# Down projections of two SwiGLU layers: eight half-block products per pair of blocks replaced by seven, operands streamed through DRAM, sums over all pairs in PSUM

## The chip, the cores and the metric

The kernel runs on one core of one Trainium2 chip. The metric is the device time of one execution in microseconds (us), the median of several runs. Beside the runs there is one profiled execution, from whose trace every duration below is read.

## The reference

The program is one layer of a streaming encoder for 1024 tokens of 1024 channels, all in 32-bit floats: a feed-forward network (FFN 1), a mixer (attention and a recurrence), and a second feed-forward network (FFN 2), each in a frame of normalisation, modulation, gate and residual.

```
D_MODEL = 1024; SEQ = 1024; D_FF = 2816; DEPTH = 1

def swiglu(h, w_gu, w_down):
    g, u = jnp.split(h @ w_gu, 2, axis=-1)
    return (jax.nn.silu(g) * u) @ w_down

def sandwich(x, fn, g_pre, g_post, shift, scale, gate, res_w):
    h = modulate(rmsnorm(x, g_pre), shift, scale)
    y = rmsnorm(fn(h), g_post)
    return x + res_w * gate[:, None, :] * y

def reference(...):
    mod = (c_act @ w_ada[l] + b_ada[l]).reshape(b, N_SUB, 3, D_MODEL)
    ...
    x = sandwich(x, ffn1, ..., 0.5)
    x = sandwich(x, mix, ..., 1.0)
    x = sandwich(x, ffn2, ..., 0.5)
```

The change concerns `act @ w_down` of the two FFNs: [1024 tokens, 2816] times [2816, 1024].

## The kernel before

**Precision.** Every operand of a product is split into two parts in the type fp32r: `hi`, a cast by ACT, and `lo = raw - hi`, a subtraction by DVE or GpSimd (POOL), in `split` (L135 to L137). A product is then three matmuls: hi x hi, hi x lo, lo x hi. A matmul here has 128 x 128 against 128 x 512 elements.

**Gate and up.** The hidden width 2816 is 22 blocks of 128 channels. The first 4 blocks of FFN 1 and the first 3 of FFN 2 are plain products. For each block after them `block` (L612) does seven products of half blocks in place of eight (Strassen's scheme: sums and differences of quarters of the operands are multiplied, and the results are added with signs). For every product `mix` (L582) makes a sum of two quarters of the weight block on GpSimd (`wsum`, L592; five of the seven need one), casts it on ACT (L595) and takes the rest on DVE (L596). This runs one block ahead: after product i of block fb, operand i of block fb+1 is prepared. DVE and ACT also move results out of PSUM (`sub_t` at L619 and others). The finished block of `act` is stored to DRAM (L648), in one transfer of 512 KB. The raw gate and up weights of the block after the next follow (L481, tiles `raw` and `sr`, 512 KB each). In FFN 1 one step of the modulation's matrix product (`bg`, the "adaLN" tiles `rawa`, 512 KB of weights each) runs after each block, since later parts of the program need its result.

**Down projection.** It takes the 22 blocks in seven chunks of 2, 4, 3, 3, 3, 4 and 3. For a chunk, `down_w` loads the activations and the weights of each block (tile `rawd`, 512 KB, L729) and splits them, the weights' remainders on GpSimd. Then, for each of 8 blocks of 128 tokens, all blocks of the chunk are multiplied into two PSUM banks `pd` (L766), of 512 output channels each. The first chunk's result is copied to `yacc` in SBUF (ACT, L777); the others are added to it by DVE (L779).

**Epilogue.** When a token block is complete, the class `Epilogue` treats it in stages. `put` sums its squares (ACT, L304), forms 1/rms (`rstd`, two small operations on GpSimd, L305 and L306) and multiplies by the gate (GpSimd, L365). `update` adds it to the residual (DVE, L371), stores it and takes the next sum of squares. `norm` (L382) normalises, and `drain` transposes the normalised tokens on PE for the next layer. `last_steps` says which stage runs at which step. The very last token block of the program goes through `push_last` (L407), which works in halves of 512 channels.

**What sets the order.** PE, DVE, ACT and GpSimd work their instructions in the order in which the code is written. A scheduler orders SP's queue, which issues all large DMAs, one behind the other: an instruction that waits on SP holds up all behind it. Tiles come from pools with a fixed number of buffers: 3 of `raw` (shared by all streamed weights and by `rawd`), 4 each of `wh` and `wl`, 22 of the general 512 KB tiles that `t4` returns, 16 of `h`. PSUM has 8 banks: 6 of the tag `ps` (`bank`) and 2 of the tag `tr` (`trbank`, for transposes).

## Time and profile before

| | |
|---|---|
| median of 3 runs | 2282.09 us |
| their range | 2281.98 to 2283.41 us |
| span of the profiled execution, first to last instruction | 2280.4 us |
| mean granted TensorE clock of that execution | 0.991 |
| moved by DMA in it | 250.31 MB, 110 GB/s on average |

The profile names an engine, a line, an operation and the tile it writes (`<-` the tiles it reads), with numbers of buffers left out. PE is TensorE's matmul, PEld its loading of weights, which overlaps with it. DVE is the vector engine, ACT the scalar engine, POOL is GpSimd, SP the engine whose queue issues the DMAs. The groups of instructions give, behind a count `x54:`, the least, median and largest duration in ns. A row of the timeline begins with the start and the duration in us; what stands in brackets at its end is the idle time of the engine just ahead of it and what ended that.

### The profile page before, as it was taken

Reading aid. Unit: us, or ns where it says so; the run is one execution under the profiler, and the core shown is the slowest. Engines: PE = TensorE matmul, PEld = TensorE weight load, DVE = VectorE, ACT = ScalarE, POOL = GpSimd, SP = SyncE. Lnnn points to the kernel's source line nnn. Section 1 sums busy time; section 2 is a strip of 40 time slices with the busy share of each in tenths; the row PEclk is TensorE's granted clock in tenths of the full one; section 3 lists DMA queues with packets and bytes.
Section 4 is the critical chain, followed back from the end, with each engine's and each line's share of the span. In section 5 each row is a group of like instructions: output and inputs, shape, how many; then the busy total and the mean of one; then the engine's idle time right before and its main releaser. Section 6 shows DMA issues by size and latency. Waiting matters only on the chain.

```text
span 2280.4 us, 26502 instructions
## 1 busy us (share of the span) xinstructions
PE 2212.2 (97%) x10227; PEld 1837.4 (81%) x10227; DVE 1277.7 (56%) x1830; ACT 925.0 (41%) x1473; POOL 638.2 (28%) x449
## 2 busy tenths in 40 slices
PE   5989999999999999999999999999989999999998
PEld 3867888888788788888898988887878888888886
DVE  6675565545755677643336666546864444433444
ACT  3533333342223587821147777336433333342121
POOL 3433333322225311000021120006443333322324
PEclk9999999999999999999999999999999999999999
DMA  9322333345663211245312011554322222233223
GB/s 297 101 65 75 111 111 102 111 146 177 195 211 120 77 50 40 66 148 166 113 51 65 25 59 53 165 176 169 113 81 83 84 82 83 84 121 110 93 93 120
DMA packets 217749, 250.31 MB, mean 110 GB/s; under 512 B 10864, under 2 KB 172824, under 8 KB 217624
## 3 DMA queue, kind: packets, MB, share of 16 engines
q1 hardware_dynamic: 217512, 248.60, 34.7%
q8 instruction: 80, 1.31, 0.2%
q14 instruction: 45, 0.37, 0.0%
q10 hardware_dynamic: 112, 0.03, 0.0%
HBM read 203.51 MB, written 48.23 MB: 110 GB/s over the span
## 4 chain that ended last, share of the span: by engine, by line
PE 80%; DVE 8%; ACT 4%; issue 3%; DMA 2%; POOL 2%; SPq 1%; POOLq 0%; DVEq 0%; ACTq 0%
PE pd L766 19%; PE pj L433 6%; PE pj L434 6%; PE pj L435 6%; PE pj L1064 5%; PE psB L603 3%; PE psB L604 3%; PE psB L605 3%; PE psC L603 3%; PE psC L604 3%; PE psC L605 3%; PE psA L603 3%; PE psA L604 3%; PE psA L605 3%; PE pv L1111 1%
## 5 line engine op out<-in xcount | busy, mean ns | idle before, releaser
L766 PE MATMUL pd<-dh,ah 128*128 128x512 f32 x1440 | 346.9, 392 | 0.0
L766 PEld LDWEIGHTS pd<-dh,ah 128*128 128x128 f32 x1440 | 271.8, 189 | 57.0 <-POOL dh L137 0.5
L434 PE MATMUL pj<-hl,wh 128*128 128x512 f32 x576 | 226.9, 394 | 5.5 <-DVE hl L316 5.5
L779 DVE TENSOR_TENSOR yacc<-yacc,pd 128x512 f32<-128x512 f32 x190 | 121.9, 683 | 193.3 <-PE pd L766 193.2
L435 PE MATMUL pj<-hh,wl 128*128 128x512 f32 x576 | 227.1, 394 | 2.6 <-DVE wl L137 1.9
L433 PE MATMUL pj<-hh,wh 128*128 128x512 f32 x576 | 229.3, 398 | 0.0
L592 POOL TENSOR_TENSOR wsum<-raw,sr 128x512 f32<-128x512 f32 x70 | 101.0, 1443 | 318.4 <-DVE wm L596 313.8
L596 DVE TENSOR_TENSOR wm<-wsum,wm 128x512 fp32r<-128x512 f32 x185 | 146.8, 804 | 61.9 <-ACT wm L595 59.2
L595 ACT CAST wm<-wsum 128x512 fp32r<-128x512 f32 x185 | 112.5, 620 | 111.3 <-PE psB L605 83.9
L137 POOL TENSOR_TENSOR wl<-raw,wh 128x1024 fp32r<-128x1024 f32 x25 | 61.2, 2454 | 292.0 <-ACT wh L136 246.7
L136 ACT CAST wh<-raw 128x1024 fp32r<-128x1024 f32 (+1 forms) x86 | 86.8, 1011 | 129.2 <-PE pj L434 53.2
L434 PEld LDWEIGHTS pj<-hl,wh 128*128 128x128 f32 x576 | 109.4, 190 | 29.3 <-DVE hl L316 7.4
L435 PEld LDWEIGHTS pj<-hh,wl 128*128 128x128 f32 x576 | 109.3, 190 | 26.9 <-DVE wl L137 3.2
L603 PE MATMUL psB<-hh,wm 128*128 128x512 f32 x296 | 117.2, 396 | 14.1 <-DVE mixes L619 14.1
L433 PEld LDWEIGHTS pj<-hh,wh 128*128 128x128 f32 x576 | 109.5, 190 | 22.1 <-ACT hh L321 0.3
L137 DVE TENSOR_TENSOR wl<-raw,wh 128x1024 fp32r<-128x1024 f32 (+1 forms) x61 | 73.8, 1211 | 84.7 <-ACT wh L136 84.7
L604 PE MATMUL psB<-hl,wm 128*128 128x512 f32 x296 | 116.8, 395 | 0.0
L605 PE MATMUL psB<-hh,wm 128*128 128x512 f32 x296 | 116.8, 394 | 0.0
L603 PE MATMUL psC<-hh,wm 128*128 128x512 f32 x296 | 115.6, 391 | 0.5 <-ACT wm L595 0.5
L605 PE MATMUL psA<-hs,wm 128*128 128x512 f32 x296 | 115.3, 389 | 0.4 <-DVE wm L596 0.4
L605 PE MATMUL psC<-hh,wm 128*128 128x512 f32 x296 | 115.3, 390 | 0.0
L603 PE MATMUL psA<-hs,wm 128*128 128x512 f32 x296 | 115.3, 389 | 0.0
(296 smaller groups left out, 5218.0 us busy)
## 6 DMA issues: line engine op xcount, KB each, us to landing
rawa<-in_w_ada_dram SPq DMA_DIRECT2D x56, 512.0 KB, 3.7
raw<-in_ffn_w_gu_dram SPq DMA_DIRECT2D x49, 512.0 KB, 4.0
rawd<-act SPq DMA_DIRECT2D x44, 512.0 KB, 4.3
rawd<-in_ffn_w_down_dram SPq DMA_DIRECT2D x44, 512.0 KB, 4.1
raw<-in_w_in_dram SPq DMA_DIRECT2D x44, 512.0 KB, 3.8
sr<-in_ffn_w_gu_dram SPq DMA_DIRECT2D x39, 512.0 KB, 5.7
act<-act SPq DMA_DIRECT2D x37, 512.0 KB, 4.2
rawa<-in_w_ada_dram SPq DMA_DIRECT2D x32, 256.0 KB, 5.6
```

What stands on the lines that cost most here:

```text
L137: (eng or nc.vector).tensor_tensor(lo, raw, hi.bitcast(F32), op=ALU.subtract)
L433: nc.tensor.matmul(dst, wh[:, kk, :], xhk[:, sl], start=first, stop=False)
L434: nc.tensor.matmul(dst, wh[:, kk, :], xlk[:, sl], start=False, stop=False)
L435: nc.tensor.matmul(dst, wl[:, kk, :], xhk[:, sl], start=False, stop=last)
L595: nc.scalar.copy(t[:, 0], src)
L596: nc.vector.tensor_tensor(t[:, 1], src, t[:, 0].bitcast(F32), op=ALU.subtract)
L603: nc.tensor.matmul(dst, t[:, 0, kk, :], xh, start=first and kk == 0, stop=False, skip_group_check=True)
L604: nc.tensor.matmul(dst, t[:, 0, kk, :], xl, start=False, stop=False, skip_group_check=True)
L605: nc.tensor.matmul(dst, t[:, 1, kk, :], xh, start=False, stop=last and kk == 3, skip_group_check=True)
L766: nc.tensor.matmul(pd[h], a_[:, tk], w_[:, h * 512 : (h + 1) * 512], start=(i == 0 and j == 0), stop=(i == n - 1 and j == 2),)
L779: nc.vector.tensor_tensor(yacc[sb][:, sl], yacc[sb][:, sl], pd[h], op=ALU.add)
L1064: nc.tensor.matmul(d, a[:, k, :], b[k][:, sl], start=k == 0 and i == 0, stop=k == KB - 1 and i == 2)
```

## The change

The down projection is now done like the gate and up products: the 22 blocks are taken as 11 pairs, and the two halves of a pair's channels, of the tokens and of the output channels make 2 x 2 blocks, so that seven products of halves stand for eight (numbered 1 to 7, in the order `STREAM`). For each product the contraction runs over all 11 pairs in PSUM: 4 banks hold 4 token blocks x 512 output channels, each bank receiving 3 matmuls of every pair. One "unit" is a tile `rawd` of 128 x 2 x 512 elements: the product's half of the activations and its half of the weights, 256 KB each, loaded by two DMAs (L789) and split by one cast and one subtraction. There are 7 x 11 = 77 units per FFN; `take` requests them three ahead.

Four of the seven products need sums or differences of `act` (rows of a pair against each other and halves of tokens), four need sums of `w_down`. `pair_sums` makes them ahead of the products: two loads of 512 KB, four additions on GpSimd of 128 x 512 elements (L756) and two stores of 512 KB into new DRAM tensors, `acts` and `downs`. `all_sums` lists them, the weights of a pair and then the activations of pairs that are complete, as a generator with a `yield` after the loads and after each addition. One step of it runs after each product of `block` (behind `mix`), the rest with the first product of the down projection.

Products 1, 6, 7 and 4 accumulate in one set of four banks (`chain`, two of them of the tag `tr`) which are read between them without being cleared, so that the next product adds to the one before; products 2, 5 and 3 have banks of their own. `reads` says which results ACT copies and DVE adds to `yacc`. In the last product the first four units are multiplied for all token blocks, while the Epilogue treats token blocks 0 to 3; the last seven units are kept in `t4` tiles and taken for one token block after the other.

```diff
-CHUNKS = (2, 4, 3, 3, 3, 4, 3)
+KEPT_FROM = 4
...
     def trbank(name):
+        if tr_home[0] == "ps":
+            return bank(name)
...
         def push_last(self, sb, y, pd):
...
-            for h, sl in enumerate(halves):
-                junk = tmp[0].tile([P, D], BF16, tag="junk", bufs=2, name=nm("junk"))
-                nc.vector.tensor_tensor(y[:, sl], y[:, sl], pd[h], op=ALU.add)
-                nc.scalar.activation(junk[:, sl], y[:, sl], AF.Square, scale=D ** -0.5, accum_out=sq[h])
-                if h == 0:
-                    nc.vector.tensor_tensor(y[:, sl], y[:, sl], g[:, sl], op=ALU.mult)
+            one = halves[1]
+            nc.scalar.activation(junk[1][:, one], y[:, one], AF.Square, scale=D ** -0.5, accum_out=sq[1])
+            nc.vector.tensor_tensor(y[:, one], y[:, one], g[:, one], op=ALU.mult)
             self.update(sb - 1)
+            one = halves[0]
+            nc.scalar.activation(junk[0][:, one], pd, AF.Square, scale=D ** -0.5, accum_out=sq[0])
+            nc.vector.tensor_tensor(y[:, one], pd, g[:, one], op=ALU.mult)
...
-            nc.vector.tensor_tensor(y[:, halves[1]], y[:, halves[1]], g[:, halves[1]], op=ALU.mult)
...
                 def after(i):
                     mix(fb + 1, i)
-                    if fb == NF - 1 and i in (6, 5, 4, 3):
-                        down_w(0, (6, 5, 4, 3).index(i))
+                    next(jobs, None)
+                    if fb == NF - 1 and i in (5, 4, 3):
+                        units.fetch((5, 4, 3).index(i) + 1)
+
+                ready[0] = fb
...
-                bg(1)
+                bg(2)
+            ready[0] = NF
...
+        def pair_sums(j, weights):
+            src, dst = (w_down, down_s) if weights else (act_d, act_s)
+            top, bot = t4("top"), t4("bot")
+            nc.sync.dma_start(top, rows(src, 2 * j))
+            nc.sync.dma_start(bot, rows(src, 2 * j + 1))
+            t1, t2, b1, b2 = top[:, h1], top[:, h2], bot[:, h1], bot[:, h2]
+            add, sub_ = ALU.add, ALU.subtract
+            yield
+            if weights:
+                steps = ((t1, t2, t1, sub_), (t2, b2, t2, sub_), (b2, b2, t1, sub_), (b1, b1, b2, sub_))
             else:
+                steps = ((b2, t2, b2, add), (t2, t1, t2, sub_), (t1, b2, t1, sub_), (b1, b1, t1, sub_))
+            for o, p, q, op in steps:
+                nc.gpsimd.tensor_tensor(o, p, q, op=op)
+                yield
+            nc.sync.dma_start(rows(dst, 2 * j), top)
+            nc.sync.dma_start(rows(dst, 2 * j + 1), bot)
...
+                    raw = wpool.tile([P, 2, 512], F32, tag="raw", bufs=3, name=nm("rawd"))
+                    for o, (t, k, half) in enumerate((act_of[p], down_of[p])):
+                        nc.sync.dma_start(raw[:, o], rows(t, 2 * j + k)[:, (h1, h2)[half]])
+                    if p == STREAM[-1] and j >= KEPT_FROM:
+                        hi, lo = t4("dh", F32R, (P, 2, 512)), t4("dl", F32R, (P, 2, 512))
+                    else:
+                        hi, lo = (wpool.tile([P, 2, 512], F32R, tag=t, bufs=4, name=nm("dh")) for t in ("wh", "wl"))
+                    split(raw, hi, lo, nc.gpsimd if self.n > 8 and self.n % 3 == 2 else nc.vector)
...
+            for p in STREAM[:-1]:
+                own = p in (1, 6, 7)
+                dst = chain if own else [bank("pv") for _ in range(4)]
+                for j in range(PAIRS):
+                    ops = units.take(p, j, 3)
+                    for i in range(half):
+                        mm(dst[i], i, ops, j == 0 and p not in (6, 7), j == PAIRS - 1)
+                    if own:
+                        next(jobs, None)
+                        next(jobs, None)
+                        bg(1)
...
+            for j in range(KEPT_FROM):
+                ops = units.take(p, j, 3)
+                for i in range(half):
+                    mm(chain[i], i, ops, False, False)
+                epi.put(j, yacc[j])
+                if j > 0:
+                    epi.update(j - 1)
+                if j > 1:
+                    epi.norm(j - 2)
+
+            last_steps = {4: ((3,), (2, 3), 2), 5: ((4,), (), 4), 6: ((5,), (4,), 2), 7: ((6,), (5,), KB)}
+            for i in range(half):
+                sb = half + i
+                for j in range(KEPT_FROM, PAIRS):
+                    mm(chain[i], i, units.take(p, j, 3), False, j == PAIRS - 1)
+                if tail and i == half - 1:
+                    epi.push_last(sb, yacc[sb], chain[i])
+                    break
+                copy(sb, h1, chain[i])
+                epi.put(sb, yacc[sb])
...
```

In the two listings of before and after below, a row is one instruction: its line, the operation, the tile with its number that it writes, and what it reads. GpSimd's queue in the gate and up blocks of FFN 2, before: the five weight sums of one block and the first of the next.

```order
L592 TENSOR_TENSOR wsum_13949<-raw_13929 128x512
L592 TENSOR_TENSOR wsum_13967<-raw_13929,sr_13931 128x512
L592 TENSOR_TENSOR wsum_14005<-sr_13931,raw_13929 128x512
L592 TENSOR_TENSOR wsum_14023<-sr_13931 128x512
L592 TENSOR_TENSOR wsum_14060<-raw_13929,sr_13931 128x512
L592 TENSOR_TENSOR wsum_14086<-raw_14066 128x512
```

And with the change (the line of the weight sums is now L598, that of the pair sums L756):

```order
L598 TENSOR_TENSOR wsum_14511<-raw_14491 128x512
L756 TENSOR_TENSOR bot_14429<-bot_14429,top_14428 128x512
L598 TENSOR_TENSOR wsum_14530<-raw_14491,sr_14493 128x512
L756 TENSOR_TENSOR top_14537<-top_14537 128x512
L598 TENSOR_TENSOR wsum_14575<-sr_14493,raw_14491 128x512
L756 TENSOR_TENSOR top_14537<-bot_14538,top_14537 128x512
L598 TENSOR_TENSOR wsum_14594<-sr_14493 128x512
L756 TENSOR_TENSOR bot_14538<-bot_14538,top_14537 128x512
L756 TENSOR_TENSOR bot_14538<-bot_14538 128x512
L598 TENSOR_TENSOR wsum_14633<-raw_14491,sr_14493 128x512
```

An addition of a pair now stands ahead of nearly every weight sum, in the same queue; the five weight sums of a block are still in their order.

SP's queue at the same place, before: per block one store of `act` and two loads of weights.

```order
L648 DMA act_11949<-act_13796 128x1024
L481 DMA sr_14068<-in_ffn_w_gu_dram 128x8x128
L481 DMA raw_14340<-in_ffn_w_gu_dram 128x8x128
L648 DMA act_11949<-act_13933 128x1024
L481 DMA sr_14205<-in_ffn_w_gu_dram 128x8x128
```

With the change (L758 and L759 store a pair's sums, L746 and L747 load the two rows of a pair, L487 loads the gate and up weights, L654 stores the block):

```order
L758 DMA acts_12139<-top_14428 128x1024
L759 DMA acts_12139<-bot_14429 128x1024
L487 DMA sr_14493<-in_ffn_w_gu_dram 128x8x128
L487 DMA raw_14794<-in_ffn_w_gu_dram 128x8x128
L654 DMA act_12138<-act_14346 128x1024
L746 DMA top_14537<-in_ffn_w_down_dram 128x1024
L747 DMA bot_14538<-in_ffn_w_down_dram 128x1024
L758 DMA downs_12140<-top_14537 128x1024
L759 DMA downs_12140<-bot_14538 128x1024
L746 DMA top_14640<-in_ffn_w_down_dram 128x1024
L747 DMA bot_14641<-in_ffn_w_down_dram 128x1024
L487 DMA sr_14647<-in_ffn_w_gu_dram 128x8x128
```

The loads of a pair stand behind the stores of the pair before and, every second or third time, behind two weight loads and the block's store; the weight loads in turn stand behind stores, which wait for GpSimd's additions.

GpSimd's queue at the end of FFN 1's down projection, before: squares and gate products of the token blocks, with no split between them.

```order
L365 TENSOR_TENSOR yacc_3710<-yacc_3710,gate_4295 128x1024
L305 TENSOR_SCALAR rstd_5128<-rstd_5128 128x1
L306 TENSOR_TENSOR rstd_5128<-rstd_5128,nhalf 128x1
L365 TENSOR_TENSOR yacc_3733<-yacc_3733,gate_4295 128x1024
L305 TENSOR_SCALAR rstd_5136<-rstd_5136 128x1
```

With the change (L309 and L310 form `rstd`, L369 is the gate product, L141 the split; `dl_5423` and `dl_5503` are the remainders of units 5 and 8 of the last product):

```order
L369 TENSOR_TENSOR yacc_4249<-yacc_4249,gate_3545 128x1024
L309 TENSOR_SCALAR rstd_5415<-rstd_5415 128x1
L310 TENSOR_TENSOR rstd_5415<-rstd_5415,nhalf 128x1
L141 TENSOR_TENSOR dl_5423<-rawd_5419,dh_5422 128x1024
...
L369 TENSOR_TENSOR yacc_4251<-yacc_4251,gate_3545 128x1024
...
L369 TENSOR_TENSOR yacc_4253<-yacc_4253,gate_3545 128x1024
L309 TENSOR_SCALAR rstd_5484<-rstd_5484 128x1
L310 TENSOR_TENSOR rstd_5484<-rstd_5484,nhalf 128x1
L141 TENSOR_TENSOR dl_5503<-rawd_5499,dh_5502 128x1024
```

Two splits that the last product's matmuls need now stand between the gate products of token blocks 0 to 3.

More of the change, by code (lines that the diff above doesn't have):

```diff
@@ new lines, in all_sums @@
+        def all_sums():
+            done = 0
+            for j in range(PAIRS):
+                yield from pair_sums(j, True)
+                while done < PAIRS and 2 * done + 2 < ready[0]:
+                    yield from pair_sums(done, False)
+                    done += 1
+            while done < PAIRS:
+                if 2 * done + 1 < ready[0]:
+                    yield from pair_sums(done, False)
+                    done += 1
+                else:
+                    yield
+        jobs = all_sums()
@@ L739, in down_phase @@
+        units = Units()
         def down_phase(make, ahead):
             epi = Epilogue(sub, xin, xout, EPS, make)
[L741 removed]
             half = SB // 2
[L743 to L752 removed]
@@ new lines, in down_phase, with mm, copy @@
+            tail = make is None
+            def mm(dst, i, ops, first, last):
+                hi, lo = ops
+                tk = slice(i * P, (i + 1) * P)
+                for n, (a_, w_) in enumerate(((hi, hi), (hi, lo), (lo, hi))):
+                    nc.tensor.matmul(
+                        dst, a_[:, 0, tk], w_[:, 1, :], start=first and n == 0, stop=last and n == 2,
+                        skip_group_check=True,
+                    )
+            yacc = {}
+            def copy(sb, sl, src):
+                if sb not in yacc:
+                    yacc[sb] = t4("yacc")
+                nc.scalar.copy(yacc[sb][:, sl], src)
```

127 lines of the change are left out of this document (53 added, 74 removed).

## The prediction

> **What bounds the kernel now.** I read the busy shares first, then the chain of work that ended last, then the stretches of the two down projections.
>
> ```profile
> PE 2212.2 (97%) x10227; PEld 1837.4 (81%) x10227; DVE 1277.7 (56%) x1830; ACT 925.0 (41%) x1473; POOL 638.2 (28%) x449
> ...
> PE 80%; DVE 8%; ACT 4%; issue 3%; DMA 2%; POOL 2%; SPq 1%; POOLq 0%; DVEq 0%; ACTq 0%
> ```
>
> TensorE (PE) is busy nearly throughout and holds 80% of the chain. The table of windows and the chain in order of time show the down projections themselves:
>
> ```profile
> 495.00:725.00 230.00, 227.55 (x1011) 188.00 (x1010) 139.16 (x152) 61.63 (x76) 70.82 (x40) 0.99 0.57 184
> 1739.00:1758.00 19.00, 19.00 (x86) 15.73 (x85) 9.22 (x14) 6.08 (x11) 6.74 (x6) 1.00 0.27 84
> 2040.00:2270.00 230.00, 230.00 (x1015) 189.99 (x1013) 95.34 (x120) 52.41 (x63) 74.33 (x41) 1.00 0.31 105
> ```
> ```profile
> 2030.57 235.17 PE pd L766 x1037
> ```
>
> After the stretch come its length, then busy time of PE, weight loads, DVE, ACT and GpSimd (POOL), the granted clock, DMA share and GB/s. The down products run without a gap, 1037 in 235.17 us, so 0.227 us each. Fewer of them is time gained, as long as nothing new makes PE wait. The second row is one 19 us block of the gate and up products: PE is full there too, and GpSimd is busy 6.74 us of 19.
>
> **What goes.** Each of the two FFNs had 22 x 8 x 2 x 3 = 1056 down products and gets 7 x 11 x 4 x 3 = 924 of the same shape. That is 264 fewer, at 0.227 us: **-59.9 us**. Everything else is cost.
>
> **Pair sums beside the gate and up blocks.** The new sums (L756 in the changed kernel) put 88 additions per FFN on GpSimd: one after each product in four products of five, in the queue that makes the weight sums of the next block. The timeline gives that queue for one block, then the ACT casts that wait for it:
>
> ```profile
> 1757.73 1.29 POOL L592 TENSOR_TENSOR wsum<-raw,sr 128x512 f32<-128x512 f32 x1 [5.18 <-DVE wm L596]
> 1760.09 1.29 POOL L592 TENSOR_TENSOR wsum<-raw 128x512 f32<-128x512 f32 x1 [1.06 <-DVE wm L596]
> 1766.05 1.29 POOL L592 TENSOR_TENSOR wsum<-raw,sr 128x512 f32<-128x512 f32 x1 [4.67 <-DVE wm L596]
> 1768.68 1.68 POOL L592 TENSOR_TENSOR wsum<-sr,raw 128x512 f32<-128x512 f32 x1 [1.34 <-DVE wm L596]
> 1770.31 1.28 POOL L592 TENSOR_TENSOR wsum<-sr 128x512 f32<-128x512 f32 x1
> ```
> ```profile
> 1774.67 0.62 ACT L595 CAST wm<-wsum 128x512 fp32r<-128x512 f32 x1
> 1777.70 0.62 ACT L595 CAST wm<-wsum 128x512 fp32r<-128x512 f32 x1 [2.41 <-PE psB L605]
> ```
>
> The sum that starts at 1768.68 ends 4.3 us ahead of its cast, the next one 6.1 us. GpSimd may be about 6 us late before anybody notices; beyond that ACT and DVE, which take their queues in order, evacuate PSUM late, and PE waits. That wait exists already at the first blocks:
>
> ```profile
> PE psB L603 <- DVE mixes L619: 14.1, 3, 6.6
> ```
>
> Now the work of a block. It has 7 products, so 7/5 = 1.4 pairs with 5.6 additions, and 5 weight sums: 10.6 x 1.29 = 13.7 us of 19.05 (84 products at 0.227). Into the rest, 5.4 us, must go two things: waits for loads, and the quarrel with DVE. The first addition of a pair waits for loads that SP issues only behind the stores of the pair before, and often behind two weight loads and the store of the block (the order above). Their durations, from the list of DMA issues and a window at the start:
>
> ```profile
> raw<-in_ffn_w_gu_dram SPq DMA_DIRECT2D x49, 512.0 KB, 4.0
> rawd<-act SPq DMA_DIRECT2D x44, 512.0 KB, 4.3
> ...
> sr<-in_ffn_w_gu_dram SPq DMA_DIRECT2D x39, 512.0 KB, 5.7
> ```
> ```profile
> 20.00:30.00 10.00, 4.64 (x14) 3.43 (x14) 7.48 (x9) 2.16 (x3) 4.50 (x2) 1.00 1.17 290
> ```
>
> A 512 KB load lands 4 us after its issue; one that is issued right behind another 1.7 us later (5.7 against 4.0), and 512 KB at 290 GB/s also take 1.8 us. So from the last addition of a pair to the first of the next: at best 4.3 us (one load), about 7 us behind a store (4.3 and the store, the second load), some 11 us behind two weight loads and a store more. One or two weight sums, 1.8 us on average, fill part of it. Per block that is 1.4 x (4.3 - 1.8) = 3.5 us at the low end and 1.4 x (6.7 - 1.8) = 6.9 us at the high one (6.7 is my mean over the orders of the pairs); I take the middle, 5.2.
>
> The quarrel is shown where GpSimd works back to back, at the start of the second FFN:
>
> ```profile
> 1613.33 2.40 POOL L527 TENSOR_TENSOR bot<-hh,hl 128x1024 f32<-128x1024 f32 x1 [4.91 <-DVE hl L316]
> ...
> 1624.10 2.85 POOL L527 TENSOR_TENSOR bot<-hh,hl 128x1024 f32<-128x1024 f32 x1
> ```
> ```profile
> 1627.42 2.89 DVE L544 TENSOR_TENSOR hs<-hsum,hs 128x512 fp32r<-128x512 f32 x1
> ...
> 1633.63 0.68 DVE L554 TENSOR_TENSOR bot<-bot,top 128x512 f32<-128x512 f32 x1
> ```
>
> A DVE operation of 0.68 us takes 2.9 us while GpSimd runs, and GpSimd's takes 2.85 instead of 2.40: about 0.4 us for each meeting. A block has 8 DVE operations on two SBUF operands; none to all of them meet GpSimd, 0 to 3.2 us, and I take half, 1.6. The sum is 13.7 + 5.2 + 1.6 = 20.5 us, 1.45 over the block. The 21 pairs that are summed in the blocks take 105 steps, 15 blocks: 15 x 1.45 = 22 us, less the 6 us of slack: **+16 us** in the second FFN. The first also moves two adaLN weight tiles per block, in the same DMA queue and through DVE; half a load (0.9 us) more per block gives 2.35 x 15 - 6 = **+29 us**. Both ends: nothing (13.7 + 3.5 = 17.2 fits), and 15 x (13.7 + 6.9 + 3.2 - 19.05) - 6 = 65 us for each.
>
> [...] If every meeting happens, the block is 22.1 us, and that is the third rival.
>
> **The first product of the first FFN** streams 11 operand tiles while 12 adaLN tiles still run between them; before, they were spread over longer steps:
>
> ```profile
> 645.00:660.00 15.00, 15.00 (x68) 12.43 (x67) 11.92 (x13) 4.22 (x4) 3.37 (x2) 1.00 0.79 252
> 660.00:675.00 15.00, 14.12 (x57) 11.54 (x56) 8.96 (x9) 5.15 (x5) 6.17 (x3) 0.77 0.67 226
> ```
>
> With the last pair and the last store it is 28 transfers of 512 KB; at 1.7 us 47.6 us of DMA. PE needs them in 30 us and the prefetch begins some 8 us ahead: **+8 us** (from 0, if enough has landed earlier, to 20 at the 226 GB/s of the second row). The other five inner products need 0.5 MB in 2.7 us, 193 GB/s, which the before ran at without PE waits; their ACT casts (1.05 of 2.72 us) and subtractions are covered by it. Cost nothing.
>
> **The last product** holds the epilogue, in 30 us instead of some 50. Its durations:
>
> ```profile
> L136 ACT CAST dh<-rawd x54: 1044/1053/1062, 477.6 to 2210.6; 128x1024 fp32r<-128x1024 f32 x54
> ...
> L137 DVE TENSOR_TENSOR ah<-rawd,ah x34: 1212/1219/3303, 500.2 to 2190.8; 128x1024 fp32r<-128x1024 f32 x34
> L137 POOL TENSOR_TENSOR dl<-rawd,dh x22: 2375/2408/3480, 486.4 to 2211.7; 128x1024 fp32r<-128x1024 f32 x22
> ```
> ```profile
> L305 POOL TENSOR_SCALAR rstd<-rstd x47: 219/426/1316, 6.7 to 2268.4; 128x1 f32<-128x1 f32 x47
> L306 POOL TENSOR_TENSOR rstd<-rstd,nhalf x47: 567/570/1673, 7.0 to 2269.4; 128x1 f32<-128x1 f32 x47
> L371 DVE SCALAR_TENSOR_TENSOR xr<-yacc,rstd,xr x15: 1272/1283/1286, 703.4 to 2273.3; 128x1024 f32<-128x1024 f32 x15
> ```
> ```profile
> L777 ACT COPY yacc<-pd x32: 589/590/592, 498.2 to 2052.6; 128x512 f32<-128x512 f32 x32
> L304 ACT ACTIVATE junk<-yacc x15: 1055/1058/1060, 698.8 to 2267.1; 128x1024 bf16<-128x1024 f32 x15
> L304 ACT ACTIVATION_READ_ACCUMULATOR junk<-yacc x15: 186/187/189, 699.8 to 2268.1; 128x1 f32 x15
> L365 POOL TENSOR_TENSOR yacc<-yacc,gate x14: 2339/2400/2419, 700.9 to 2269.9; 128x1024 f32<-128x1024 f32 x14
> L382 DVE TENSOR_SCALAR yacc<-xr,rstd x8: 745/761/2866, 710.9 to 770.1; 128x1024 f32<-128x1024 f32 x8
> ...
> L419 DVE TENSOR_TENSOR yacc<-yacc,gate x1: 2143/2143/2143, 2270.7 to 2270.7; 128x512 f32<-128x512 f32 x1
> ```
>
> Count from its first matmul. PE passes four units (10.9 us), then takes the last seven for one token block at 0.68 us each: unit 8 is due at 13.6 and that block ends at 15.7. GpSimd has ahead of unit 8's subtraction (first FFN): four puts of 0.43 + 0.57 + 2.40 = 3.4, three updates of 1.0, unit 5's subtraction and its own, 2.4 each: 21.4 us. It begins at 2.3, after a cast and a square (1.05 + 1.06 + 0.19), and ends at 23.7. Unit 10's buffer is free when unit 7 is cut at about 20.7, behind an update that waits for GpSimd; load 4.3, cast, subtraction: 27.3. The token block ends at 27.7, 12 us late. The transposes right behind it wait for copy 0.59, square 1.25, put 3.4, update 1.0, normalisation 0.76: 7 us. **+19 us**. In the second FFN no update runs on GpSimd, but half of unit 8's load stands behind a store that waits for an update (16.2): load, cast, subtraction give 24, unit 10 24.4, the token block 24.9: **+9 us**. The rest of the epilogue follows at PE's pace. Bounds: 5 less each if the queues meet better, 8 more each if loads queue as above. The final block no longer has the 2.14 us multiplication on its way to the end: **-2 us** (0 to -4).
>
> **Clock.** In the window 660 to 675 above PE sat idle for 0.9 us, the granted clock fell to 0.77 and 57 matmuls were done instead of 68: 11 x 0.227 = 2.5 us, 1.6 beyond the idle time. Three long waits: **+5 us**. [...]
>
> **Sum.** -59.9 + 16 + 29 + 8 + 19 + 9 - 2 + 5 = +24 us on a span of 2280.4: 2304; the runs' median (2282.09) lies 1.7 above that execution: **2306 us**.
>
> **Rivals.** Forecast (58%): GpSimd sets the pace of the blocks. First rival, on the other side (27%): the loads land early enough, a block's GpSimd work fits into 19.05 us, and the pair sums cost nothing: 2306 - 45 = 2261. For it speaks the 12 us that GpSimd is idle in a block now; against it that SP has the loads behind stores that wait for GpSimd itself. It decides at 5.4 us of waits and meetings per block. Second (5%): the last and first products hide their waits too: 2261 - 33 = 2228. Third (10%): every meeting and the long waits: up to 65 in place of 16 and 29: 2306 + 85 = 2391 at the most, half of it 2348. That the products aren't fewer is out: the order has 264 PE rows less.
>
> **Numbers.** A measurement of this kernel tells about 0.2% from no change, 2277.5 to 2286.7. The forecast's own spread, some 25 us, puts 0.05 of its 0.58 below and 0.06 within; the first rival 0.25 and 0.02. Faster 0.35, same 0.08, slower 0.57. The range runs from below the first rival's price to the middle of the third's: 2250 to 2365.
>
> **What would show it.** Right: in the blocks POOL is over 85% busy or waits for the DMAs of top and bot, blocks take 20 to 21 us, and PE waits for mixes or wm; two waits near the first FFN's last product, one of 9 us in the second's. Wrong: blocks of 19.1 us, or no PE wait for dl; then a term above is hidden.

## The result, and the profile after

The changed kernel takes **2391.48 us** (median of 4 runs, 2391.02 to 2392.31) against 2282.75 us of the kernel before (4 runs): 1.0478 times as long, 95% interval 1.0466 to 1.0491. The profiled execution spans 2390.5 us, 110 us more than the 2280.4 before. The forecast was 2306, range 2250 to 2365: the direction is right, the time lies outside the range, and close to the third rival's upper end (2391).

The busy shares and the chain of the changed kernel:

```profile
PE 2201.8 (92%) x9963; PEld 1813.3 (76%) x9963; DVE 1335.8 (56%) x1740; ACT 997.9 (42%) x1538; POOL 896.2 (37%) x621
...
PE 55%; DMA 13%; POOL 11%; DVE 9%; ACT 5%; issue 5%; SPq 2%; POOLq 0%; DVEq 0%; ACTq 0%
```

There are 264 matmuls fewer, as the change says, but PE is busy only 10.4 us less instead of 59.9. Its share of the chain falls from 80% to 55%, and DMA and GpSimd now hold 24%. What PE waits for, the largest rows and those that the text needs (engine, tile and line, what ended the wait; total us, times, longest):

```profile
PE psB L609 <- DVE mixes L625: 72.0, 23, 7.0
PE pc L204 <- DVE acc L191: 18.7, 3, 9.3
PE px L813 <- ACT dh L140: 10.8, 3, 5.0
PE px L813 <- POOL dl L141: 10.8, 4, 4.7
...
PE pb L134 <- DMA rowsB<-in_lru_lambda_dram: 7.7, 1, 7.7
...
PE px L813 <- DVE dl L141: 5.9, 3, 4.2
...
PE pt L339 <- DVE yacc L386: 6.3, 1, 6.3
```

In the kernel before, the first of these rows was 14.1 us. The stages, read off the starts of PE's matmuls by their tiles (us; a product of 132 matmuls at 0.227 us is 29.9):

| stage | before | after |
|---|---|---|
| FFN 1, 16 steps from a seven-product block to the next | 319.2 | 383.1 |
| FFN 1, first three down products | | 50.0, 33.5, 38.6 |
| FFN 1, first down matmul to the first seven-product block of FFN 2 | 1164.9 | 1178.5 |
| FFN 2, 17 such steps | 331.9 | 379.5 |
| FFN 2, last down product | | 45.2 |
| FFN 2, first down matmul to the end | 249.9 | 232.8 |

The steps differ by +63.9, +13.6, +47.6 and -17.1; with 2 us in the stretches between, that is the 110. The gain is there: in FFN 2 six of the seven down products run at 29.9 us each, full (first row below: stretch, its length, PE, weight loads, DVE, ACT, POOL busy, clock, DMA share, GB/s). The seventh is not (second row), nor is the down projection of FFN 1 as a whole (third row):

```profile
2157.60:2337.10 179.50, 179.50 (x794) 148.63 (x793) 73.62 (x65) 76.06 (x79) 53.88 (x24) 1.00 0.63 206
2337.10:2382.30 45.20, 33.74 (x132) 25.57 (x131) 20.70 (x15) 18.31 (x27) 32.34 (x24) 0.85 0.55 190
561.40:834.00 272.60, 233.68 (x989) 189.39 (x988) 122.03 (x108) 109.44 (x129) 92.02 (x57) 0.91 0.63 206
```

**The blocks.** The 16 blocks of FFN 2 from the second on, before and after, in the same columns:

```profile
1687.70:1992.30 304.60, 304.60 (x1345) 252.33 (x1344) 147.57 (x225) 97.34 (x176) 108.46 (x80) 1.00 0.28 83
```
```profile
1767.30:2119.50 352.20, 321.62 (x1346) 261.05 (x1345) 191.06 (x225) 100.47 (x176) 224.63 (x157) 0.96 0.56 186
```

A block takes 352.2 / 16 = 22.0 us instead of 19.04. GpSimd's waits in those 16 blocks after the change, then ACT's largest, then what SP waits for longest:

```profile
POOL bot L756 <- DMA bot<-act: 42.3, 8, 7.3
POOL wsum L598 <- DMA sr<-in_ffn_w_gu_dram: 37.7, 11, 6.4
POOL top L756 <- DMA top<-in_ffn_w_down_dram: 21.2, 7, 3.4
POOL wsum L598 <- DVE wm L602: 18.2, 10, 4.7
POOL top L756 <- DMA bot<-in_ffn_w_down_dram: 3.2, 3, 1.6
```
```profile
ACT wm L601 <- POOL wsum L598: 157.7, 56, 7.4
```
```profile
SPq L758 <- POOL top L756: 122.4, 19, 10.9
SPq L759 <- POOL bot L756: 66.2, 19, 5.9
```

Per block GpSimd works 14.0 us, waits 4.2 for the loads of a pair (`top`, `bot`), 2.4 for the weights `sr`, 1.1 for DVE and 0.2 for its own issue: 21.9 of 22.0. ACT waits 157.7 us for GpSimd's weight sums, 9.9 per block. And SP stands for 188.6 of the 352.2 us before stores (L758, L759) whose sums GpSimd has not finished. One stall step by step, first the queue of SP (start, us, what it issues), then one row each of GpSimd, ACT, DVE and PE:

```profile
1843.78 0.78 SPq L747 DMA_DIRECT2D bot<-act  x1
1856.38 0.32 SPq L758 DMA_DIRECT2D acts<-top  x1
1859.78 0.32 SPq L759 DMA_DIRECT2D acts<-bot  x1
1860.15 0.43 SPq L487 DMA_DIRECT2D sr<-in_ffn_w_gu_dram  x1
```
```profile
1865.03 1.27 POOL L598 TENSOR_TENSOR wsum<-raw,sr 128x512 f32<-128x512 f32 x1 [3.57 <-DMA sr<-in_ffn_w_gu_dram]
```
```profile
1866.33 0.62 ACT L601 CAST wm<-wsum 128x512 fp32r<-128x512 f32 x1 [4.22 <-POOL wsum L598]
```
```profile
1867.59 0.68 DVE L625 TENSOR_TENSOR mixes<-psB,mixes 128x512 f32<-128x512 f32 x1
```
```profile
1868.42 0.47 PE L609 MATMUL psB<-hh,wm 128*128 128x512 f32 x1 [2.95 <-DVE mixes L625]
```

From 1844.6 to 1859.8 SP stands, but for the 0.3 us that issue the first, before two stores that wait for GpSimd's additions; these had themselves to wait for the load of `bot`, until 1850.85. Behind the stores stands the load of `sr`, which GpSimd needs next. GpSimd starts on it 4.9 us after its issue; the weight sum, its cast, the remainder and, behind it in DVE's queue, the evacuation of `psB` are all late, and PE stands for 2.95 us. GpSimd holds up its own load. And the stall goes on after its end:

```profile
1865.00:1869.90 4.90, 1.95 (x10) 1.31 (x9) 1.99 (x3) 1.48 (x3) 1.53 (x2) 1.00 0.99 372
1869.90:1873.30 3.40, 3.40 (x10) 2.63 (x9) 1.89 (x2) 0.25 (x1) 3.32 (x3) 0.50 0.03 12
```

For the next 3.4 us the granted clock is 0.50: 8 matmuls start, 0.43 us apart (the row's 10 count two that began before it), instead of 15 at 0.227 us, which is 1.6 us lost. Nine gaps of PE in FFN 2's blocks, of 2.1 to 6.5 us, are each followed by such a stretch, of 3.4 or 6.8 us; a tenth, of 2.0 us, is not.

### The profile page after: what moved, and what is told of

The parts are those of the page before. It is cut to its first block, busy times and chain, and to the rows that moved or that the text cites. A ratio compares the mean times of both kernels' runs of the same rounds, so it can differ in the third digit from the quotient of the medians.

```text
span 2390.5 us, 27027 instructions
## 1 busy us (share of the span) xinstructions
PE 2201.8 (92%) x9963; PEld 1813.3 (76%) x9963; DVE 1335.8 (56%) x1740; ACT 997.9 (42%) x1538; POOL 896.2 (37%) x621
## 4 chain that ended last, share of the span: by engine, by line
PE 55%; DMA 13%; POOL 11%; DVE 9%; ACT 5%; issue 5%; SPq 2%; POOLq 0%; DVEq 0%; ACTq 0%
PE px L813 7%; PE pv L813 6%; PE pj L437 6%; PE pj L438 6%; PE pj L439 6%; PE pj L1150 5%; POOL wsum L598 3%; POOL bot L756 3%; DMA sr<-in_ffn_w_gu_dram 2%; POOL top L756 2%; DMA bot<-act 2%; DMA rawa<-in_w_ada_dram 2%; PE pv L1197 1%; DMA top<-in_ffn_w_down_dram 1%; DVE wm L602 1%
## 5 line engine op out<-in xcount | busy, mean ns | idle before, releaser
L602 DVE TENSOR_TENSOR wm<-wsum,wm 128x512 fp32r<-128x512 f32 x185 | 174.6, 952 | 177.3 <-ACT wm L601 176.2
L140 ACT CAST dh<-rawd 128x1024 fp32r<-128x1024 f32 x154 | 161.8, 1052 | 263.7 <-PE pv L813 69.0
L141 DVE TENSOR_TENSOR dh<-rawd,dh 128x1024 fp32r<-128x1024 f32 x100 | 131.0, 1312 | 230.5 <-ACT dh L140 230.4
L609 PE MATMUL psB<-hh,wm 128*128 128x512 f32 x296 | 128.4, 434 | 72.0 <-DVE mixes L625 72.0
L141 POOL TENSOR_TENSOR dh<-rawd,dh 128x1024 fp32r<-128x1024 f32 x40 | 96.0, 2400 | 260.2 <-ACT dh L140 260.2
L813 PE MATMUL px<-dh,dh 128*128 128x512 f32 x592 | 186.3, 396 | 1.1 <-DVE dh L141 1.1
L141 POOL TENSOR_TENSOR wl<-raw,wh 128x1024 fp32r<-128x1024 f32 x25 | 61.3, 2459 | 291.2 <-ACT wh L140 246.2
L813 PE MATMUL pv<-dh,dh 128*128 128x512 f32 x528 | 162.9, 389 | 2.2 <-POOL dh L141 1.4
L813 PE MATMUL px<-dh 128*128 128x512 f32 x352 | 142.8, 406 | 10.8 <-ACT dh L140 10.8
L598 POOL TENSOR_TENSOR wsum<-raw,sr 128x512 f32<-128x512 f32 x70 | 104.9, 1498 | 113.2 <-DMA sr<-in_ffn_w_gu_dram 71.7
L813 PEld LDWEIGHTS px<-dh,dh 128*128 128x128 f32 x592 | 113.9, 193 | 25.5 <-DVE dh L141 1.5
L609 PEld LDWEIGHTS psB<-hh,wm 128*128 128x128 f32 x296 | 61.5, 208 | 94.4 <-issue 81.7
L141 DVE TENSOR_TENSOR wl<-raw,wh 128x1024 fp32r<-128x1024 f32 (+1 forms) x61 | 76.1, 1249 | 89.8 <-ACT wh L140 89.8
```

Source lines behind the costliest of these rows:

```text
L140: nc.scalar.copy(hi, raw)
L141: (eng or nc.vector).tensor_tensor(lo, raw, hi.bitcast(F32), op=ALU.subtract)
L598: nc.gpsimd.tensor_tensor(src, p, q, op=op)
L602: nc.vector.tensor_tensor(t[:, 1], src, t[:, 0].bitcast(F32), op=ALU.subtract)
L609: nc.tensor.matmul(dst, t[:, 0, kk, :], xh, start=first and kk == 0, stop=False, skip_group_check=True)
L813: nc.tensor.matmul(dst, a_[:, 0, tk], w_[:, 1, :], start=first and n == 0, stop=last and n == 2, skip_group_check=True,)
```

## The experiments

In the code changes below, `...` stands for lines left out. Three theories on the blocks. **Q**: GpSimd waits for loads that stand in SP's queue behind stores, and those wait for GpSimd. **W**: GpSimd's added work and its meetings with DVE fill the block. **T**: the added bytes delay the loads. Times are medians beside 2282 to 2284 us of the kernel before on the same chip, with ratio and 95% interval.

**e1_no_sums.** `jobs` is empty, and the products read `act_d` and `w_down`.

```diff
...
-        jobs = all_sums()
+        jobs = iter(())
```

> Left out: all pair sums (their loads, additions and stores); the products read halves of act and of w_down in their place, so traffic and matmuls of the down projection itself stay. The blocks of gate and up cost 64 us (first FFN) and 48 us (second) more in the changed kernel than before. If the pair sums are the whole reason, the blocks go back to 19.0 us each and the time falls by 112 us and some 10 us more in the first product, to about 2270 us. If two steps of adaLN per block or something else in the blocks takes part, the first FFN's blocks stay above 20 us and the time above 2300.

2300.64 us (1.0075, 1.0046 to 1.0104), the second of the two cases. The 17 steps of FFN 2 are back to 333.5, but the 16 of FFN 1 take 341.0, not 319.2. So the pair sums cost 46 us in FFN 2 and 42 in FFN 1; another 22 us in FFN 1 come from something else, and of the down projection's losses nearly all stay (first three products 44.0, 35.8 and 36.7; last of FFN 2 47.7).

**e2_traffic_only.**

```diff
-            for o, p, q, op in steps:
-                nc.gpsimd.tensor_tensor(o, p, q, op=op)
+            for _ in steps:
                 yield
```

> Left out: the additions of the pair sums; their loads and stores stay, with nothing between. Theory Q (SP's queue: GpSimd waits for loads that stand behind stores which wait for GpSimd) and theory W (GpSimd's own work and its meetings with DVE fill the blocks) both expect the blocks near 19.0 us, since no store waits for GpSimd and GpSimd has no additions: 2270 to 2290 us. Theory T (the added bytes alone delay the weight loads): blocks stay above 20 us, over 2330 us.

2296.83 us (1.0060, 1.0037 to 1.0083), 7 us above the range given, since FFN 1 keeps what e1 left open; 340.1 and 331.6 us in the blocks, as in e1. All loads and stores of the sums are there and cost the blocks nothing. T falls.

**e3_apart.**

```diff
-                nc.gpsimd.tensor_tensor(o, p, q, op=op)
+                nc.gpsimd.tensor_tensor(own[0][:, h1], own[0][:, h2], own[0][:, h2], op=op)
...
```

> The loads and stores of the pair sums stay, with nothing between them, and GpSimd makes the same number of additions of the same size at the same places, but on a tile of its own that is loaded once: work and traffic of the changed kernel, without the dependence of one on the other (the sums are not formed). Theory Q: blocks near 19 to 19.5 us, 2275 to 2310 us. Theory W: the blocks stay at 20 to 22 us, 2360 us or more.

2300.64 us (1.0074, 1.0048 to 1.0100); 344.2 and 331.2 us. This number of additions and this traffic, without the dependence, are nearly free. In the 16 blocks of FFN 2 GpSimd now waits for nothing but DVE, which means that it is ahead:

```profile
POOL wsum L598 <- DVE wm L602: 111.8, 54, 5.2
```

W does not fall by this alone: an addition on the tile of its own, which reads one operand twice, takes 1.09 us, and GpSimd works 189.0 us in these blocks instead of the changed kernel's 224.6. The full work comes in e5.

```profile
L756 POOL TENSOR_TENSOR own<-own 128x512 f32<-128x512 f32 x75 | 81.8, 1090 | 1.3
```

**e4_ahead.** The pair's loads move in front of the additions of the pair ahead of it.

```diff
+            nxt = choose()
+            while nxt or todo[False] < PAIRS:
+                cur, nxt = nxt, choose()
+                yield
+                if cur:
+                    yield from pair_sums(*cur)
...
```

> Nothing left out. The loads of a pair are issued before the additions of the pair ahead of it, instead of behind its stores; activations go before weights where both are there. Theory Q: GpSimd's waits for top and bot (64 us in the second FFN's blocks, 43 in the first's) go, those for sr (38 and 34), which still stand behind stores, stay in part: 2310 to 2345 us. Theory W: within 10 us of 2391.

2354.80 us (1.0312, 1.0282 to 1.0342): two fifths of the way from 2391 to 2300, in the direction of Q, though 10 us more than I gave it. In FFN 2 the 17 steps are 349.1; in FFN 1 374.7. In the 16 blocks of FFN 2 the waits for the pairs fall from 66.7 to 8.2 us, and the wait for `sr` has grown from 37.7 to 55.4, since the stores still stand ahead of it:

```profile
POOL wsum L598 <- DMA sr<-in_ffn_w_gu_dram: 55.4, 14, 10.7
POOL bot L757 <- DMA bot<-act: 8.2, 2, 5.2
```

**e5_act_stores.** e4, and a pair's stores leave from ACT's queue, two products after the last addition.

```diff
-            nc.sync.dma_start(rows(dst, 2 * j), top)
-            nc.sync.dma_start(rows(dst, 2 * j + 1), bot)
+                nc.scalar.dma_start(rows(dst, 2 * j), top)
+                nc.scalar.dma_start(rows(dst, 2 * j + 1), bot)
...
```

> As e4 (loads one pair ahead), and the stores of the pair sums are issued by ACT, two products after their last addition, so that no store in SP's queue waits for GpSimd. Theory Q: GpSimd's waits for sr (58 us in e4's second FFN blocks) go too, the 17 blocks of the second FFN take 331 to 336 us (349 in e4), the 16 of the first 340 to 348 (375), and the time is 2298 to 2315 us, the level of e1 to e3. Rival: the stores only move the wait to ACT, which then casts and evacuates late: blocks stay above 20 us, 2340 or more.

2312.26 us (1.0123, 1.0094 to 1.0153): 331.1 us in FFN 2 and 348.6 in FFN 1, within a us of what Q gave. The 16 blocks of FFN 2:

```profile
1729.50:2034.10 304.60, 304.60 (x1346) 252.30 (x1345) 195.42 (x225) 98.91 (x176) 222.17 (x156) 1.00 0.61 207
```

GpSimd makes the same operations as in the changed kernel (156 against 157) in nearly the same time, 1.42 and 1.43 us each; in the blocks before it was 1.36. DVE makes 225 operations in all three, in 147.6 us before, 191.1 after the change and 195.4 here. So the whole work and the meetings with DVE are there, and PE is full, at 19.04 us per block: W falls. **Q is shown** in FFN 2, where the pair sums cost nothing now: their price was the order of stores and loads in one queue. From the changed kernel to e5 the steps of the two FFNs lose 34.5 and 48.4 us. Of the 12 us by which e5 lies above e1, 8 are in FFN 1's steps and 5 in FFN 2's first down product (34.8 us). The stores on ACT's queue without the earlier loads were not run.

**e6_last.** The last product alone; the updates, normalisations and transposes of the steps behind it are shifted to match.

```diff
-... nc.gpsimd if self.n > 8 and self.n % 3 == 2 else nc.vector)
+... nc.gpsimd if self.n > 8 and self.n % 3 == 2 and p != STREAM[-1] else nc.vector)
-                ops = units.take(p, j, 3)
+                ops = units.take(p, j, 3 + 2 * j)
-                if j > 0:
-                    epi.update(j - 1)
                 if j > 1:
-                    epi.norm(j - 2)
+                    epi.update(j - 2)
...
```

> The changed kernel with another last product: all its splits on DVE, its units requested up to seven ahead, and updates and normalisations of token blocks 0 to 3 one to two steps later. If the wait for units 5 to 10 (splits behind gate products on GpSimd, loads behind stores that wait for updates) is what makes the two last products 60.5 and 45.2 us, they become some 48 and 33 us, and the time 2362 to 2372 us. If the epilogue's own work sets their length, the waits move behind the last matmuls and the time falls by less than 8 us.

2381.08 us (1.0425, 1.0394 to 1.0455), 10 us less; expected were 19 to 29. FFN 2's last product falls from 45.2 to 34.4 us, as expected, but the time from the last matmul to the end rises from 8.1 to 15.2. In FFN 1 the product falls by 4.7 (60.6, with transposes, to 55.9). PE's waits in the tile `px` fall from 28.6 to 12.2 us, those for the normalised tokens rise from 6.3 to 10.6:

```profile
PE pt L339 <- DVE yacc L386: 10.6, 3, 5.8
PE px L813 <- ACT dh L140: 5.6, 4, 2.6
PE px L813 <- DVE dl L141: 5.2, 8, 1.1
PE px L813 <- DVE dh L141: 1.4, 1, 1.4
```

Both theories are half right: the units waited as I said, and behind them stands the epilogue's own chain.

**e7_spread.** The two adaLN steps of a block apart.

```diff
+                    if i in (4, 7):
+                        bg(1)
-                bg(2)
```

> The changed kernel with its two adaLN steps per block apart: one after product 4, one after product 7, instead of both at the block's end. If the short distance between a load or a sum and the PE instruction that needs it is the reason (PE waits of 18.7 us for acc and 7.7 us for rowsB), these waits fall below 8 us in all; the blocks of the first FFN get 10 to 22 us shorter, as far as GpSimd's waits do not hide it: 2368 to 2382 us. If adaLN costs by its work on DVE or its bytes, nothing changes: within 5 us of 2391.

2386.50 us (1.0448, 1.0418 to 1.0479), where the other theory put it. PE's waits for `rowsB` and for adaLN sums in the blocks are gone, but FFN 1's steps are only 6.6 us shorter (376.5), since PE now waits there longer for `mixes` (45.8 us, 34.9 before the edit); and in the first down product one adaLN sum still holds PE for 13.7 us.

**e8_all.** e5, e6 and e7 together.

> e5, e6 and e7 together. If the three losses are separate, their gains add: 2300 to 2315 less 20 to 28 for the last products less 10 to 20 for adaLN, 2252 to 2285 us; what is then left over 2222 (the time before less 60) is the first product and the first block.

2274.65 us (0.9965, 0.9945 to 0.9984), inside the range. With GpSimd in time, the spread of e7 is worth 22 us: FFN 1's steps go from 348.6 in e5 to 326.3, 7 above the kernel before. Work and bytes are the same in both, so these 22 us are the two adaLN steps taken back to back. (The same background queue `bg` also brings `rowsB`, parameters of the mixer.) In e5's steps PE waits 4.0 us for `rowsB`, 5.0 for an adaLN sum and 5.6 for the two parts of another, and is busy 7.9 us longer than in e8, whose PE has none of these waits. That these are the 22 us which e1 left open is likely, since size and place agree; e1 with the steps apart was not run. The last 7 us stay open.

**e10_bg_later.** The changed kernel, with no adaLN step in the first down product; they follow from the second on, one in three units.

```diff
                         next(jobs, None)
+                    if p != 1 and j % 3 == 1:
                         bg(1)
```

> The changed kernel, with no adaLN step in the first product of the down projection; from the second product on one follows every third unit. If the adaLN tiles (their turns in the DMA queue, in the three raw buffers and on PE) make the first three products of the first FFN 50.0, 33.5 and 38.6 us, these become 30 to 36 us each and the time 2364 to 2376 us. If the pair sums and operands alone do it, the three stay above 40, 33 and 33 us, and the time within 8 us of 2391.

2385.20 us (1.0449, 1.0428 to 1.0470), less gain than expected. The first product falls from 50.0 to 35.5, as the first theory has it, the next two are 32.0 and 36.8, but the fourth and fifth rise from 29.9 to 36.5 and 34.8. So 14.5 us of the first product come with the adaLN steps, and most of the cost follows them to wherever they go.

**e9_best.** e8 with that, and the sums of the last pair at one step per unit, through the first two products.

> e8 with the adaLN steps of e10, and with the last pair's sums at one step per unit through the first two products, so that ACT's store does not wait for a pair just loaded (ACT idle for 10.6 us behind GpSimd in e8's second FFN, whose first product is 34.8 us). The first three products of the first FFN fall from 45.7, 35.0 and 38.7 us to 30 to 35 each, the first of the second to 30: 2243 to 2260 us against 2274.65. If the operands' own loads set the first product, 2262 or more.

2266.24 us (0.9933, 0.9916 to 0.9949), 6 us above the range given. The first products of FFN 1 and 2 are 30.9 and 29.9, as expected; the second to fifth of FFN 1 are 34.2, 36.3, 36.8 and 36.6.

**e11_rawa.** e9 with adaLN tiles of the down projection in the general buffers.

```diff
-            raw = wpool.tile([P, 1024], F32, tag="raw", bufs=3, name=nm("rawa"))
+            raw = t4("rawa") if ada_home[0] == "t4" else wpool.tile([P, 1024], F32, tag="raw", bufs=3, name=nm("rawa"))
```

> e9, with the adaLN tiles of the down projection in the general tiles instead of in the three raw buffers that the operands use. In e9 the second to fifth product of the first FFN take 34.2, 36.3, 36.8 and 36.6 us and a unit's chain (issue, load of 3 to 6 us, cast, subtraction) holds its raw buffer for 8 to 10 us, about three units of 2.72 us. If a raw buffer lent to adaLN is what the units lack, the four fall to 30 to 32 us and the time to 2242 to 2254 us. If the DMA's bytes or DVE's time set them, they stay above 33 us and the time above 2258.

2250.54 us (0.9862, 0.9843 to 0.9880), inside the range of the buffer theory. Three of the four products fall as expected: they are 30.4, 39.3, 29.9 and 31.8. DMA moves more, not less, in the same stretch, e9 first, then e11:

```profile
530.00:590.00 60.00, 56.16 (x248) 44.31 (x246) 28.18 (x22) 21.11 (x23) 15.75 (x7) 1.00 0.67 216
```
```profile
530.00:590.00 60.00, 57.07 (x239) 46.77 (x239) 26.11 (x23) 21.80 (x23) 16.69 (x7) 0.91 0.88 290
```

So 216 GB/s was no limit, and a lent raw buffer was what the units of three products lacked. The third product does not wait for a unit at all. Its row, and PE's only wait in it:

```profile
564.40:603.60 39.20, 36.49 (x150) 30.07 (x149) 18.16 (x17) 14.28 (x16) 10.88 (x5) 0.87 0.84 273
```
```profile
PE pc L206 <- DVE yacc L845: 2.7, 1, 2.7
```

The matmuls of an adaLN step (`pc`) wait for a DVE addition that reads a result of the second product; in the down projection `pc` takes its PSUM bank from the same six as the products, so it is probably the bank that they wait for. The row's mean granted clock is 0.87, from which I estimate about 5 us more (0.13 x 39.2).

**e12_kept.** e11 with `KEPT_FROM = 5`, the updates and normalisations shifted to match.

> e11, with five units instead of four taken for all token blocks ahead of those kept in the last product. If the last products (55.7 and 37.4 us in e9) still wait for the kept units' loads and splits, 2.7 us more of cover shorten each by 2 to 5 us: 3 to 10 us below e11. If they wait for the epilogue (residual tiles, normalisation), nothing is gained: within 3 us of e11, or some us slower.

2250.22 us (0.9853, 0.9836 to 0.9869), the same as e11. The last products are 4.7 and 4.8 us shorter (52.4 and 32.4), and the tail is 5.3 longer (16.8): as in e6, the epilogue ends last. e11 and e12 beat both kernels, 1.4 to 1.5% faster than the one before, with intervals clear of 1.

## Why the prediction was wrong, step by step

**Right.** The products: 29.9 us each where nothing else interferes, so -59.9 was there to be had. The final block, -2: the end after the start of the last matmul is 8.1 us, 10.8 before. That GpSimd becomes the bound of the blocks, through loads behind stores. That this alone decides between faster and slower is not borne out: without any pair sums, e1 is still 0.75% slower than the kernel before. Of the signs named, PE's waits for `mixes` and `dl` and GpSimd's for `top` and `bot` are there; the blocks are longer than the 20 to 21 us given.

The terms beside -59.9, and what the stages show for them (us; the clock's +5 has no stage of its own):

| term | forecast | measured |
|---|---|---|
| FFN 2, steps of the blocks | +16 | +47.6 |
| FFN 1, steps of the blocks | +29 | +63.9 |
| FFN 1, first down product | +8 | +20.1 |
| FFN 1, second and third | 0 | +3.6, +8.7 |
| FFN 1, last product and what follows, up to FFN 2 | +19 | +11 |
| FFN 2, last product | +9 | +15.3 |
| final block | -2 | -2.7 |

**The term of the pair sums: the step that failed.** Forecast for GpSimd were 20.5 us per block: 13.7 of work, 1.6 of meetings with DVE, 5.2 of waits for the loads of a pair. Work and meetings measure 14.0, and the waits for `top` and `bot` 4.2, inside the stated 3.5 to 6.9. What the sum put at nothing is the other half of the loop: the weights `sr` stand behind the same stores, and GpSimd waits for them 2.4 us per block. It also waits 1.1 us for DVE: it can prepare only as many sums as `wsum` has buffers (2), so time in which it is ahead isn't saved for a later wait. With 0.2 of its own issue that makes 22.0 us, 2.96 over the old block instead of 1.45. That the waits for loads are 6.5 in all, near the 5.2, is luck. "The 6 us of slack" were a second mistake, taken off the sum once but seen nowhere: the third seven-product block of FFN 2 takes 24.1 us already. 16 x 2.96 = 47 stands against +16 in FFN 2. In FFN 1 the pair sums cost 42 (e1) against the same 16; the other 13 of the +29 stood for adaLN.

The meetings were put on the wrong engine. Their price is DVE's: its 225 operations take 43.5 us more in the 16 blocks, 2.7 per block, and e5 shows that DVE has room for it.

**AdaLN in the blocks had the wrong cause.** Half a load (0.9 us) more per block, 13 us in all, was my price for the adaLN tiles in FFN 1. The size is 22 us, and the reason another one, the distance: two steps in a row put a load and the PE instruction that needs it next to each other (e8 against e5). I had counted transfers and DVE's time, not which engine stands waiting in order.

**The first product, +8**, became 20.1, and the next two, "cost nothing", 3.6 and 8.7. The +8 had bounds of 0 and 20, so the size was near the upper one; the step that failed is the choice of the DMA's bandwidth as the limit. The rows of the changed kernel for the first three products, then PE's largest wait in them, then what SP waits for longest in the first:

```profile
561.40:611.50 50.10, 37.05 (x150) 30.14 (x149) 26.58 (x23) 10.03 (x10) 9.21 (x5) 0.83 0.76 259
611.50:645.00 33.50, 30.77 (x133) 24.58 (x132) 12.21 (x10) 15.60 (x17) 8.53 (x4) 1.00 0.72 230
645.00:683.60 38.60, 35.19 (x149) 28.93 (x148) 16.52 (x16) 12.99 (x15) 9.47 (x5) 0.91 0.65 204
```
```profile
PE pc L204 <- DVE acc L191: 12.7, 2, 9.3
```
```profile
SPq L758 <- POOL top L756: 6.7, 1, 6.7
SPq L789 <- DVE dh L141: 6.5, 4, 2.6
```

In the first product PE stands for 13.0 us, 9.3 of them for one adaLN sum. The two tiles that this sum lacked were loaded only at 580.48 and 582.31, right behind the stores of the last pair (577.82 and 580.05): the loop of the blocks again, with PE waiting. Removing it alone gains little: in e5 the product is 48.9 us. Beside the 8.5 us before those two stores, SP stands in this product for 21.5 us before loads whose `raw` buffer is still in use. e10 shows that 14.5 us come with the adaLN steps. e9 and e11 show the shared buffers as the reason for the second, fourth and fifth product; for the first no run separates the buffers from the steps' other costs.

**The last product: +9 in FFN 2 became 15.3,** 11.5 us of PE's waits and 3.8 at the lower clock. The mechanism was the one described, with the row as named: the second half of unit 8's load behind a store that waits for an update.

```profile
2351.73 0.37 SPq L789 DMA_DIRECT2D rawd<-act  x1
...
2356.49 0.34 SPq L376 DMA_DIRECT2D out_dram<-xr  x1
2356.87 0.43 SPq L789 DMA_DIRECT2D rawd<-downs  x1
```

The store was due at 16.2 us after the product's first matmul and left at 19.4. GpSimd's small operations were the mis-sized term; I had taken the medians, 0.43 and 0.57. Two of the three pairs ahead of the store ran beside DVE operations of 128 x 1024 and took 2.5 us each instead of 1.0; the second of them:

```profile
2350.26 1.08 POOL L309 TENSOR_SCALAR rstd<-rstd 128x1 f32<-128x1 f32 x1
2351.42 1.40 POOL L310 TENSOR_TENSOR rstd<-rstd,nhalf 128x1 f32<-128x1 f32 x1
```

In FFN 1, +19 was too much: the stretch from its down projection's start to FFN 2 is 13.6 us longer, which with -29.9 for the products and 32.4 for the first three leaves 11. And behind the units stands the epilogue, which the prediction let follow at PE's pace: in e6 the units come nearly in time, and 7 of FFN 2's 11 us come back as a longer end.

**The clock, +5.** PE is busy 2201.8 us where 2212.2 - 59.9 = 2152.3 were due: 49.5 us. Instead of my three long waits the trace has 25 stretches at the clock 0.50 ahead of the program's end, against 6 before. PE is busy for 113 us of all such stretches, 29 before, and half of the difference, 42 us, is my estimate of the clock's part. It does not add to the stages above, which contain it; how much of it falls into time in which PE would have waited for GpSimd anyway is not measured.

**The rivals.** The third (10%) gave 2348 to 2391 by every meeting with DVE and long waits. The time is the one, by luck; the mechanism is only half right, since e5 has the meetings and 19.04 us blocks. The first (27%) had the pair sums cost nothing: in FFN 2 another order of the same DMAs makes that true, but its 2261 would not have come out, since the other terms were too small: e1 has no pair sums and takes 2300.64. The second's 33 is less than the 8 + 19 + 9 = 36 that it drops, a slip without weight.

## What to carry to other kernels

A store that waits for an engine does not belong ahead of a load that the same engine waits for: in one in-order queue the pair is a loop, and its price in the blocks here was 83 us, of the 88 that the pair sums cost, against a gain of 60. Put such stores on another queue, and issue the loads one round earlier, before looking for faster additions: the earlier loads alone gave 37 us of the time, both together 79. When you price waits behind such a store, count every load in the queue, not only those of the new work. And price a new user of a small ring of buffers by what it takes from the others (here one of three, for some 6 us at a time: in e9 a `rawa` is issued at 536.79 and read by 543.15), and background steps by the distance between a load and its use, not by their bytes.

## What was not expected of the hardware

GpSimd's operations of 128 x 512 took 1.42 us on average beside DVE's in e5, 1.36 in the blocks before, while DVE's took 0.87 us instead of 0.66. So DVE paid for most of the meetings, and the block paid nothing.

The granted clock also fell to 0.50 after short gaps of PE. In the kernel before, a gap of 0.88 us at 665.7 and nine matmuls of 128 x 1 elements behind it (1.16 us) stand ahead of 6.8 us at 0.50, from 667.7 on. In FFN 2's blocks after the change, gaps of 2.09 and 2.95 us were followed by 3.4 us at 0.50, while one of 2.0 us was followed by none. What decides between them the runs do not show. In the stretch at 1869.90, where PE had work throughout, the 3.4 us at 0.50 cost 1.6 us.
